# Second layer's attention on one Trainium2 core: scalings behind a tile's exponentials, five output rows begun, token sums behind the last addition

## The chip, the core and the metric

The kernel runs on one core of a Trainium2 chip. A core has a matrix engine (TensorE, PE in the profile, with its weight loads as PEld), a vector engine (VectorE, DVE), an activation engine (ScalarE, ACT), GpSimd (POOL) and a queue for transfers (SyncE, SP). Each takes its own instructions in the order in which the program lists them and waits for the others through semaphores. Matrix products go to PSUM, eight banks of 128 partitions by 512 float32 numbers; everything else that the engines work on lies in SBUF.

The metric is the device time of one execution in microseconds (us). The kernel before takes 1174.16 us, the median of 3 runs (1173.87 to 1174.22).

## What is computed

A trunk of two layers over 512 tokens of width 1024 that also attends to 256 memory tokens. The first layer is a gated DeltaNet, the second a sliding-window attention with one sink logit per head (12 heads of 64, 2 shared key/value heads, window 128). Both layers add the attention to the memory (4 heads), an output projection and a SwiGLU feed-forward block. The change touches the second layer only:

```python
def sliding_window_attention(q, k, v, sinks):
    ...
    s = jnp.where(mask[None, :, None, None], s, -jnp.inf)
    m = jnp.maximum(jnp.max(s, axis=-1, keepdims=True), sink)
    p = jnp.exp(s - m)
    p = (p / (jnp.sum(p, axis=-1, keepdims=True) + jnp.exp(sink - m))).astype(v.dtype)
    o = jnp.einsum("bnhgqk,bnkhd->bnqhgd", p, vw)
...
        x = x + jnp.concatenate([mix_out, mem_o], axis=-1) @ w_out[layer]
        x = x + swiglu(rms_norm(x, ln_ffn[layer]), w_gate_up[layer], w_down[layer])
```

## The kernel before

All activations are kept transposed, as 8 tiles of 128 features by 512 tokens. Each float32 product is made of three products of numbers in a reduced format: a tile is split into a high part (`hi`, `h`, `whi`, a rounding copy on ACT) and a low part (`lo`, `l`, `wlo`, a subtraction on DVE), and `mm3` issues high x high, high x low and low x high. A projection to 128 features is eight `mm3`, so 24 matmuls of 512 columns. Its weights come as one 512 KB transfer into `wraw` (two buffers), which both halves of the split then read.

**The attention tiles** (`swa`, line 1120). Two heads make a tile: tiles 0 to 5 are the windowed heads, 6 and 7 the memory heads. For each tile `queries` projects and rotates the queries, `scores` multiplies them with the keys into PSUM banks `qk` and takes mask and maximum out of them on DVE (line 750), `softmax` makes the exponentials on ACT (line 784) and the reciprocal of their sum `den` (line 787), `weighed` scales the probabilities `sm` by it (lines 805 and 807: of the four token blocks n, the odd ones on ACT, the even ones on DVE), transposes them on PE into PSUM banks `pt`, copies these to `pf`, multiplies them with the values into another `pt` bank `o`, and `split` (line 849) makes the pair `h`, `l` of the result. The loop at line 1205 runs as a software pipeline: in turn t the scores of tile t, the transposes and values of the tile two turns earlier, the exponentials of the tile between, and, cut into pieces of 2, 3 and 4 `mm3` between them, the projection of the queries two turns ahead or, from turn 4 on, the first pieces of an output row.

**The output rows** (`row`, `output`, lines 852 and 862). Row m is one projection of the eight tiles `mix` to features m. Rows 0 to 3 are begun inside the attention (`rows`), in the banks `pj`, `pj` and the two halves of one `qk` tile; each lacks its last piece until tile 5 is done. Rows 4 to 7 run behind them. After each row DVE adds it to the residual `x[m]`, ACT and DVE make the pair `h`, `l` for the feed-forward block, and the squares are accumulated (`sq`, `sqa`).

**The start of the feed-forward block** (`ffn`, line 879). `gate(0)` and a second projection read all eight pairs; two more gates follow. `token_sums` (line 995) makes four sets of sums of the x tiles (`fc`, `raw`, then the split `T`) that `quarters` (line 1019) needs for the rest of the block; for its weights `quarters` also loads `ws` tiles and adds to them by transfers that POOL issues.

**What sets the order.** A scheduler merges the calls into one list per engine, by the order in which they are written and by what each waits for; `nosync` adds an order between two instructions without a semaphore. Pools decide which buffer a tile gets: `pj`, `qk` and `pt` have two each in the second layer's attention, taken in turn, and a new user of a buffer waits for the last reader of the old tile.

Of the kernel before, what the change touches and what calls it, by code (L numbers as in the profile page):

```python
# [85 lines left out]
class Builder:  # L86
    def __init__(self, tc, a):
        self.tc, self.nc, self.a = tc, tc.nc, a
        self.n = 0
        self.valued, self.turned = None, [None, None]  # L90
        self.table, self.table_ins, self.table_users = None, None, []
# [630 lines left out]
    def scores(self, pool, q, kk, win):  # L722
# [6 lines left out]
        mx, den, nm = (self.t(pool, [P, 2 * NC], F32, t, 3 if own else 2) for t in ("mx", "den", "nm"))  # L729
        for n0 in range(0, NC, 2):  # L730
# [14 lines left out]
            for b in range(2):  # L745
                i = b * NC + n0
                if win:
                    for n in (n0, n0 + 1):
                        c0 = 0 if n else P
                        nc.vector.tensor_tensor_reduce(  # L750
                            out=sm[n][:, b, c0:], in0=ps[b][:, n - n0, c0:], in1=self.band[:, c0:], scale=1.0,
                            scalar=NEG, op0=ALU.add, op1=ALU.max, accum_out=mx[:, b * NC + n:b * NC + n + 1])
# [7 lines left out]
        return sm, mx, den, nm  # L760

    def weigh(self, pool, scores, vv, m, out, sinks):
        self.softmax(pool, scores, sinks)
        for _ in self.weighed(pool, scores, vv, m, out, sinks is not None):
            pass

    def softmax(self, pool, scores, sinks):

        nc = self.nc
        win = sinks is not None  # L770
        sm, mx, den, nm = scores
        if win:
# [4 lines left out]
            es = self.t(pool, [P, 2 * NC], F32, "es", 2)  # L777
            self.tt(nc.vector, v4(es), v4(nm), sk, ALU.add)
            self.fn(es, es, AF.Exp)
            for n in range(NC):  # L780
                c0 = 0 if n else P
                for b in range(2):
                    i = b * NC + n
                    self.fn(sm[n][:, b, c0:], sm[n][:, b, c0:], AF.Exp, scale=0.125, bias=nm[:, i:i + 1],
                            accum_out=den[:, i:i + 1])
            self.tt(nc.vector, den, den, es, ALU.add)
        nc.vector.reciprocal(den, den)

    def weighed(self, pool, scores, vv, m, out, win):
# [4 lines left out]
        sm, mx, den, nm = scores  # L794
        o = None if own else self.bank("sc")
        group = NC if own else 2
        for n in range(NC):
# [3 lines left out]
            p = sm[n][:, :, k0 * P:]  # L801
            dn = den.rearrange("p (b n) -> p n b", b=2)[:, n, :]
            for b in range(2):
                if n % 2:
                    ins = nc.scalar.activation(p[:, b], p[:, b], AF.Copy, scale=dn[:, b:b + 1]).ins  # L805
                else:
# [496 lines left out]
```

## Time and profile before

| | |
|---|---|
| median of 3 runs | 1174.16 us |
| the profiled execution, whole | 1174.01 us |
| its span from first to last instruction | 1171.8 us |
| PE busy, DVE busy, ACT busy, POOL busy | 98%, 71%, 54%, 7% |
| second layer's scores to last values | about 696 to 782 us |
| rest of the output rows | about 782 to 809 us |
| feed-forward block of the second layer | from 814 us |

The table's times are from the start of the span. A view by time lists an instruction's start, its length, engine, line, operation and tiles, and in brackets how long its engine had been idle and which instruction of another engine ended that. Ends of matmuls are modelled and overlap the next start, so for PE the distance from start to start is the better measure of what a matmul costs. `PEclk` in a view by stretches is the granted TensorE clock, 1.00 being full speed.

### The profile page before, as it was taken

To read this page: it belongs to the slowest core of one execution; us is meant where nothing else is said; L and a number is where in the kernel's file an instruction comes from. 1 tells how busy PE (TensorE), PEld (TensorE's weight loads), DVE (VectorE), ACT (ScalarE), POOL (GpSimd) and SP (SyncE) were. 2 spreads that over 40 slices of the span, in tenths; PEclk is the share of its full clock that TensorE was granted. 3 is DMA by queue.
4 is the path that set the end of the run, shared out by engine and by line. 5 is a ranking of instruction groups with operands and counts; after the bars stand their busy time and mean duration, and the time that the engine had idled before them with its cause. 6 is when DMAs were issued, how large, how long until landed. Compare 5 with 4: busy or idle time off the path is not lost.

```text
span 1171.8 us, 19281 instructions
## 1 busy us (share of the span) xinstructions
PE 1143.1 (98%) x7330; PEld 995.9 (85%) x7330; DVE 832.6 (71%) x1558; ACT 628.9 (54%) x1250; POOL 83.0 (7%) x93
## 2 busy tenths in 40 slices
PE   7999999999999999999999999998999999999997
PEld 6888777877899998899988786776899988999986
DVE  5654877767788976488955777748798734889644
ACT  7579572366466642266643557844566522566433
POOL 0210000000111101012000000001011000111000
PEclk9999999999999999999999999998999999999998
DMA  8434341324657636377533421116377633676232
GB/s 305 124 111 117 127 118 65 101 79 162 187 136 184 157 109 167 105 180 185 135 86 99 133 65 55 55 30 187 96 183 187 158 99 106 161 176 164 84 99 83
DMA packets 72943, 151.20 MB, mean 129 GB/s; under 512 B 16732, under 2 KB 19444, under 8 KB 72852
## 3 DMA queue, kind: packets, MB, share of 16 engines
q1 hardware_dynamic: 61908, 130.06, 35.5%
q0 software_dynamic: 10944, 19.93, 10.9%
q8 instruction: 57, 0.93, 0.3%
q14 instruction: 34, 0.28, 0.1%
HBM read 143.00 MB, written 6.96 MB: 128 GB/s over the span
## 4 chain that ended last, share of the span: by engine, by line
PE 86%; DVE 8%; ACT 4%; DMA 1%; issue 1%; SPq 0%; DVEq 0%; ACTq 0%
PE pj L144 40%; PE g L144 38%; PE sc L144 5%; DVE wlo L151 2%; ACT sm L132 1%; DVE sm L750 1%; PE qk L144 1%; PE g L148 1%; DMA wraw<-in_wgu 1%; PE pt L144 1%; DMA wraw<-in_wmk 1%; PE pt L148 1%; ACT sm L805 1%; DVE qv L154 1%; DVE q L151 0%
## 5 line engine op out<-in xcount | busy, mean ns | idle before, releaser
L138 ACT ACTIVATE whi<-wraw 128x512 fp32r<-128x512 f32 (+2 forms) x324 | 241.9, 753 | 270.9 <-PE pj L144 162.6
L151 DVE TENSOR_TENSOR wlo<-wraw,whi 128x512 fp32r<-128x512 f32 (+2 forms) x324 | 270.5, 843 | 109.3 <-ACT whi L138 103.9
L144 PE MATMUL pj<-h,whi 128*128 128x512 f32 (+1 forms) x668 | 264.6, 397 | 6.1 <-DVE x L151 5.2
L144 PE MATMUL pj<-l,whi 128*128 128x512 f32 (+1 forms) x668 | 262.3, 393 | 0.0
L144 PE MATMUL pj<-h,wlo 128*128 128x512 f32 (+1 forms) x668 | 261.3, 391 | 0.0
L144 PE MATMUL g<-T,whi 128*128 128x256 f32 x1216 | 220.5, 282 | 0.0
L144 PEld LDWEIGHTS g<-T,whi 128*128 128x128 f32 x1216 | 187.0, 189 | 1.1 <-DVE fu L154 1.1
L144 PE MATMUL g<-T,wlo 128*128 128x256 f32 x608 | 171.1, 281 | 0.0
L144 PEld LDWEIGHTS pj<-h,whi 128*128 128x128 f32 x668 | 125.7, 189 | 35.2 <-issue 9.4
L144 PEld LDWEIGHTS pj<-h,wlo 128*128 128x128 f32 x668 | 126.0, 189 | 26.3 <-issue 0.9
L144 PEld LDWEIGHTS pj<-l,whi 128*128 128x128 f32 x668 | 126.0, 189 | 25.4 <-issue 0.9
L144 PE MATMUL g<-h,whi 128*128 128x256 f32 (+1 forms) x500 | 146.5, 293 | 0.0
L144 PE MATMUL g<-h,wlo 128*128 128x256 f32 (+1 forms) x500 | 145.8, 292 | 0.0
L144 PE MATMUL g<-l,whi 128*128 128x256 f32 (+1 forms) x500 | 145.5, 291 | 0.0
L144 PEld LDWEIGHTS g<-T,wlo 128*128 128x128 f32 x608 | 114.4, 188 | 0.0
L144 PEld LDWEIGHTS g<-h,whi 128*128 128x128 f32 x500 | 95.0, 190 | 2.3 <-issue 0.5
L144 PEld LDWEIGHTS g<-l,whi 128*128 128x128 f32 x500 | 94.9, 190 | 2.3 <-issue 0.5
L144 PEld LDWEIGHTS g<-h,wlo 128*128 128x128 f32 x500 | 95.0, 190 | 1.7
L1028 POOL DMA_DIRECT2D ws<-in_wgu x38 | 33.1, 872 | 744.6 <-ACT h L138 245.2
L138 ACT ACTIVATE whi<-ws 128x512 fp32r<-128x512 f32 x76 | 48.0, 631 | 49.3 <-PE g L144 41.3
L151 DVE TENSOR_TENSOR fu<-pj,rstd 128x512 f32<-128x512 f32 (+1 forms) x34 | 22.4, 660 | 52.8 <-PE pj L144 52.8
L151 DVE TENSOR_TENSOR wlo<-ws,whi 128x512 fp32r<-128x512 f32 x76 | 52.1, 686 | 7.3 <-ACT whi L138 7.2
(375 smaller groups left out, 1666.1 us busy)
## 6 DMA issues: line engine op xcount, KB each, us to landing
wraw<-in_wgu SPq DMA_DIRECT2D x50, 512.0 KB, 4.2
ws<-in_wgu SPq DMA_DIRECT2D x76, 256.0 KB, 3.6
ws<-in_wgu POOLq DMA_DIRECT2D x76, 256.0 KB, 4.8
wraw<-in_win SPq DMA_DIRECT2D x26, 512.0 KB, 3.6
wraw<-in_wdn SPq DMA_DIRECT2D x32, 384.0 KB, 3.1
wraw<-in_wdn SPq DMA_DIRECT2D x32, 320.0 KB, 2.9
wraw<-in_wgu SPq DMA_DIRECT2D x38, 256.0 KB, 4.5
wraw<-in_wout SPq DMA_DIRECT2D x16, 512.0 KB, 3.5
```

The lines of the kernel that those rows point to most:

```text
L132: ins = self.nc.scalar.activation(out, in_, func, **kw).ins
L138: self.copied = self.nc.scalar.activation(out, in_, AF.Copy, **kw).ins
L144: return self.nc.tensor.matmul(out, lhsT, rhs, start=start, stop=stop, skip_group_check=more).ins
L148: return self.nc.tensor.transpose(out, in_, self.ident[:k, :k]).ins
L151: return eng.tensor_tensor(out=out, in0=a, in1=b, op=op).ins
L154: self.nc.vector.scalar_tensor_tensor(out=out, in0=in0, scalar=scalar, in1=in1, op0=op0, op1=op1)
L750: nc.vector.tensor_tensor_reduce(out=sm[n][:, b, c0:], in0=ps[b][:, n - n0, c0:], in1=self.band[:, c0:], scale=1.0, scalar=NEG, op0=ALU.ad ...
L805: ins = nc.scalar.activation(p[:, b], p[:, b], AF.Copy, scale=dn[:, b:b + 1]).ins
L1028: nc.gpsimd.dma_start(s1, a22, accum_op=ALU.add)
```

## The change

It does four things.

1. `softmax` now also takes the reciprocals and issues all scalings (the new method `scale`) right behind a tile's exponentials, instead of `weighed` doing them just ahead of the transposes in the next turn. The small steps between maximum and exponentials (`mx`, `nm`, `es`) move to the end of `scores`.
2. `weighed` no longer splits its result. The new `settle` does it behind the next `softmax`, with the subtraction that makes `l` ordered behind the last scaling on DVE. Exponentials are ordered behind the copies of the transposes (`turned`).
3. Five output rows are begun instead of four: rows 2 and 3 share one `qk` tile, row 4 has half of another, and rows 3 and 4 have weight buffers of their own (`oh`, `ol`). From row 4 on, the weights of the next row are loaded and split ahead of the addition of the present one.
4. The token sums 1 to 3 are ordered behind the last row's addition (`ended`), and the transfers of `quarters` behind the last row's weights (`behind`).

```diff
@@ split and load
-        self.tt(eng or self.nc.vector, lo, src, hi.bitcast(F32), ALU.subtract)
+        self.low = self.tt(eng or self.nc.vector, lo, src, hi.bitcast(F32), ALU.subtract)
...
-        self.nc.sync.dma_start(raw, src)
+        self.loaded = self.nc.sync.dma_start(raw, src).ins
@@ softmax and scale
+            first = self.fn(es, es, AF.Exp)
             for n in range(NC):
                 c0 = 0 if n else P
                 for b in range(2):
                     i = b * NC + n
-                    self.fn(sm[n][:, b, c0:], sm[n][:, b, c0:], AF.Exp, scale=0.125, bias=nm[:, i:i + 1],
-                            accum_out=den[:, i:i + 1])
+                    ins = self.fn(sm[n][:, b, c0:], sm[n][:, b, c0:], AF.Exp, scale=0.125, bias=nm[:, i:i + 1],
+                                  accum_out=den[:, i:i + 1])
+                    self.nosync(ins, first)
+                    if self.turned:
+                        self.nosync(ins, self.turned[n > 1 or n + b > 1])
             self.tt(nc.vector, den, den, es, ALU.add)
         nc.vector.reciprocal(den, den)
+        if "pt" in self.pbufs:
+            for n in range(NC):
+                self.scale(sm, den, n, win)
+
+    def scale(self, sm, den, n, win):
+        p = sm[n][:, :, P if win and n == 0 else 0:]
+        dn = den.rearrange("p (b n) -> p n b", b=2)[:, n, :]
+        for b in range(2):
+            if n % 2:
+                self.copy(p[:, b], p[:, b], scale=dn[:, b:b + 1])
+            else:
+                self.scaled = self.nc.vector.tensor_scalar(
+                    out=p[:, b], in0=p[:, b], scalar1=dn[:, b:b + 1], scalar2=None, op0=ALU.mult).ins
@@ weighed
-            for b in range(2):
-                if n % 2:
-                    ins = nc.scalar.activation(p[:, b], p[:, b], AF.Copy, scale=dn[:, b:b + 1]).ins
-                else:
-                    ins = nc.vector.tensor_scalar(out=p[:, b], in0=p[:, b], scalar1=dn[:, b:b + 1], scalar2=None, op0=ALU.mult).ins
...
+            if not own:
+                self.scale(sm, den, n, win)
...
-        self.split(o, *out)
+        self.ready = o
+        if not own:
+            self.split(o, *out)
@@ output
+        w = None
         for m in range(KD):
-            ps = list(begun[m] if m < len(begun) else self.row(layer, m, mix, lambda: bank(m)))[-1]
-            self.tt(nc.vector, self.x[m], ps, self.x[m], ALU.add)
+            ps = list(begun[m] if m < len(begun) else self.row(layer, m, mix, lambda: bank(m), w))[-1]
+            ahead = bool(begun) and len(begun) <= m + 1 < KD
+            w = self.weight(a["wout"][layer, m + 1]) if ahead else None
+            self.ended = nc.vector.tensor_tensor(out=self.x[m], in0=ps, in1=self.x[m], op=ALU.add).ins
+            if ahead:
+                self.nosync(self.ended, self.low)
...
+        self.behind = self.loaded if layer else None
@@ token_sums
-        self.ts(c, x0[:, q:], g0, ALU.mult)
+        ins = nc.vector.tensor_scalar(out=c, in0=x0[:, q:], scalar1=g0, scalar2=None, op0=ALU.mult).ins
+        if layer and j:
+
+            self.nosync(ins, self.ended)
@@ quarters
-        nc.sync.dma_start(s1, a21)
-        nc.sync.dma_start(s3, a11)
+        for to, part in ((s1, a21), (s3, a11)):
+            ins = nc.sync.dma_start(to, part).ins
+            if self.behind is not None:
+                self.nosync(ins, self.behind)
@@ swa
+        def settle(o, out):
+
+            hi, lo = out
+            self.copy(hi, o)
+            self.nosync(nc.vector.tensor_tensor(out=lo, in0=o, in1=hi, op=ALU.subtract).ins, self.scaled)
...
-        own = dict(pool=sp, tags=("oh", "ol"), bufs=1)
-        rows = [self.row(1, m, mix, (lambda: self.bank("pj")) if m < 2 else (lambda m=m: half(m - 2)),
-                         **(own if m == 3 else {})) for m in range(4)]
+        rows = [self.row(1, m, mix, (lambda: self.bank("pj")) if m < 2 else half,
+                         **(dict(pool=sp, tags=("oh", "ol"), bufs=2) if m > 2 else {})) for m in range(5)]
...
-            beside((6, 7, 0, 1, 2, 3)[t], *(some(work, i) if i < 4 else work for i in n))
+            o = beside((6, 7, 0, 1, 2, 3)[t], *(some(work, i) if i < 4 else work for i in n))
             softmax((7, 0, 1, 2, 3, 4)[t])
-        beside(4, some(rows[0], 2), some(rows[1], 2), some(rows[2], 3))
+            settle(*o)
+        o = beside(4, some(rows[0], 2), some(rows[1], 2), some(rows[2], 3))
         softmax(5)
-        for m, n in ((2, 3), (3, 3)):
+        settle(*o)
+        for m, n in ((2, 3), (3, 4)):
             list(some(rows[m], n))
-        beside(5, some(rows[3], 3), [list(some(rows[m], 1)) for m in range(2)], some(rows[2], 1))
+        settle(*beside(5, some(rows[3], 2), some(rows[4], 3), (next(rows[m]) for m in (4, 4, 4, 0, 1))))
+        for m in range(2, 5):
+            list(some(rows[m], 1))
```

The instructions are the same but for their order. The next listings show it at three places. All three are DVE's list; a row has the line, the operation, the tile written and the tiles read.

The first place is turn 3 of the loop, from the rotation of the last queries (`rs`, `q`) to the subtraction `l` that frees the `pt` bank. Before:

```order
L826 COPY pf_7494<-pt_7489 128x512
L1115 STREAM_SHUFFLE rs_7506<-pj_7446 128x512
L151 TENSOR_TENSOR q_7505<-pj_7446,cosT_2749 128x512
L151 TENSOR_TENSOR rs_7506<-rs_7506,sinT_2750 128x512
L807 TENSOR_SCALAR sm_7287<-sm_7287,den_7290 128x128
L151 TENSOR_TENSOR q_7505<-q_7505,rs_7506 128x512
L151 TENSOR_TENSOR l_7439<-pt_7511,h_7438 128x512
```

After, in the same turn (`ol` and `wlo` are low halves of output weights, `den` the sum of the exponentials):

```order
L838 COPY pf_7502<-pt_7497 128x512
L1142 STREAM_SHUFFLE rs_7514<-pj_7462 128x512
L151 TENSOR_TENSOR q_7513<-pj_7462,cosT_2749 128x512
L151 TENSOR_TENSOR rs_7514<-rs_7514,sinT_2750 128x512
L151 TENSOR_TENSOR den_7302<-den_7302,es_7304 128x8
L151 TENSOR_TENSOR wlo_7818<-wraw_7815,whi_7817 128x1024
L151 TENSOR_TENSOR q_7513<-q_7513,rs_7514 128x512
L794 RECIPROCAL den_7302<-den_7302 128x8
L151 TENSOR_TENSOR ol_7917<-wraw_7914,oh_7916 128x1024
L806 TENSOR_SCALAR sm_7299<-sm_7299,den_7302 128x128 x2
L806 TENSOR_SCALAR sm_7300<-sm_7300,den_7302 128x256 x2
L1213 TENSOR_TENSOR l_7455<-pt_7519,h_7454 128x512
```

Sum, two splits of weights, reciprocal and four scalings now stand between the rotation and `l`. In turns 1 and 2 the list is the same without the row of `ol`.

The second place is behind the last values, where the rows are added to x. Before (`wlo_8006`, `wlo_8046` and `wlo_8086` are the low halves for rows 4, 5 and 6; x_535 is x[0] and so on):

```order
L151 TENSOR_TENSOR wlo_8006<-wraw_8003,whi_8005 128x1024
L154 SCALAR_TENSOR_TENSOR l_7959<-x_535_2732,gains_67,h_7958 128x512
L154 SCALAR_TENSOR_TENSOR l_7969<-x_536_2733,gains_67,h_7968 128x512
L151 TENSOR_TENSOR sqa_7974<-sq_7962,sq_7972 128x512
L154 SCALAR_TENSOR_TENSOR l_7981<-x_537_2734,gains_67,h_7980 128x512
L151 TENSOR_TENSOR x_538_2735<-qk_7817,x_538_2735 128x512
L151 TENSOR_TENSOR sqa_7986<-sqa_7974,sq_7984 128x512
L151 TENSOR_TENSOR wlo_8046<-wraw_8043,whi_8045 128x1024
L154 SCALAR_TENSOR_TENSOR l_7996<-x_538_2735,gains_67,h_7995 128x512
L151 TENSOR_TENSOR sqa_8001<-sqa_7986,sq_7999 128x512
L151 TENSOR_TENSOR x_539_2736<-pj_8009,x_539_2736 128x512
L151 TENSOR_TENSOR wlo_8086<-wraw_8083,whi_8085 128x1024
```

After (ahead of the first row stand x[0], x[1], `wlo_8037` for row 5 and the `l` of x[0]; `wlo_8077` is the low half for row 6):

```order
L889 TENSOR_TENSOR x_537_2734<-qk_7821,x_537_2734 128x512
L154 SCALAR_TENSOR_TENSOR l_8000<-x_536_2733,gains_67,h_7999 128x512
L151 TENSOR_TENSOR sqa_8005<-sq_7993,sq_8003 128x512
L154 SCALAR_TENSOR_TENSOR l_8012<-x_537_2734,gains_67,h_8011 128x512
L889 TENSOR_TENSOR x_538_2735<-qk_7821,x_538_2735 128x512
L151 TENSOR_TENSOR sqa_8017<-sqa_8005,sq_8015 128x512
L889 TENSOR_TENSOR x_539_2736<-qk_7920,x_539_2736 128x512
L154 SCALAR_TENSOR_TENSOR l_8024<-x_538_2735,gains_67,h_8023 128x512
L151 TENSOR_TENSOR sqa_8029<-sqa_8017,sq_8027 128x512
L154 SCALAR_TENSOR_TENSOR l_8042<-x_539_2736,gains_67,h_8041 128x512
L151 TENSOR_TENSOR sqa_8047<-sqa_8029,sq_8045 128x512
L151 TENSOR_TENSOR wlo_8077<-wraw_8074,whi_8076 128x1024
```

Between the low halves of two rows stood at most six other rows, and now between those of rows 5 and 6 stand twelve: the `l` of x[0] and the eleven above.

The third place is the last row's addition (x_542). Before:

```order
L151 TENSOR_TENSOR x_541_2738<-pj_8089,x_541_2738 128x512
L151 TENSOR_TENSOR T_8257<-raw_8250,T_8256 128x1024
L151 TENSOR_TENSOR wlo_8214<-wraw_8211,whi_8213 128x1024
L154 SCALAR_TENSOR_TENSOR l_8116<-x_541_2738,gains_67,h_8115 128x512
L151 TENSOR_TENSOR sqa_8121<-sqa_8081,sq_8119 128x512
L154 SCALAR_TENSOR_TENSOR raw_8261<-x_536_2733,gains_67,fc_8260 128x256
L154 SCALAR_TENSOR_TENSOR raw_8261<-x_540_2737,gains_67,fc_8260 128x256
L154 SCALAR_TENSOR_TENSOR raw_8261<-x_540_2737,minus_8247,raw_8261 128x256
L158 TENSOR_SCALAR fc_8305<-x_537_2734,gains_67 128x256
L151 TENSOR_TENSOR x_542_2739<-pj_8129,x_542_2739 128x512
```

After (`wlo_8174` is the low half for `gate(0)`, `wlo_8214` that for the projection behind it):

```order
L151 TENSOR_TENSOR wlo_8174<-wraw_8171,whi_8173 128x1024
L889 TENSOR_TENSOR x_541_2738<-pj_8089,x_541_2738 128x512
L151 TENSOR_TENSOR wlo_8214<-wraw_8211,whi_8213 128x1024
L154 SCALAR_TENSOR_TENSOR l_8122<-x_541_2738,gains_67,h_8121 128x512
L151 TENSOR_TENSOR sqa_8127<-sqa_8087,sq_8125 128x512
L154 SCALAR_TENSOR_TENSOR raw_8250<-x_539_2736,minus_8247,raw_8250 128x256
L889 TENSOR_TENSOR x_542_2739<-pj_8129,x_542_2739 128x512
L151 TENSOR_TENSOR T_8257<-raw_8250,T_8256 128x1024
L154 SCALAR_TENSOR_TENSOR l_8156<-x_542_2739,gains_67,h_8155 128x512
L151 TENSOR_TENSOR sqa_8161<-sqa_8127,sq_8159 128x512
```

The second set of token sums (`raw_8261`) has left the stretch ahead of the last addition, and the split `T` of the first set stands behind that addition. On SP's list the transfer of the last row's weights has moved from behind four `ws` transfers and one of `wraw` to ahead of them.

More of the change, by code (lines that the diff above doesn't have):

```diff
@@ L89, in __init__ @@
         self.n = 0
-        self.valued, self.turned = None, [None, None]
+        self.valued, self.turned, self.scaled, self.behind = None, [], None, None
         self.table, self.table_ins, self.table_users = None, None, []
@@ L1030, in quarters @@
         last = self.t(fp, [P, T], F32, "wraw", 2)
-        nc.sync.dma_start(last, a22)
+        ins = nc.sync.dma_start(last, a22).ins
+        if self.behind is not None:
+            self.nosync(ins, self.behind)
         pa, pb, pc = (self.bank("g")[:, :q] for _ in range(3))
```

67 lines of the change are left out of this document (33 added, 34 removed).

## Prediction

> **What bounds the kernel now.** I read the page first, then who waited for whom, then the engines' lists in order of time around the longest waits.
>
> ```profile
> PE 1143.1 (98%) x7330; PEld 995.9 (85%) x7330; DVE 832.6 (71%) x1558; ACT 628.9 (54%) x1250; POOL 83.0 (7%) x93
> PE 86%; DVE 8%; ACT 4%; DMA 1%; issue 1%; SPq 0%; DVEq 0%; ACTq 0%
> PE pj L144 <- DVE x L151: 5.2, 1, 5.2
> PE pt L148 <- ACT sm L805: 2.5, 5, 0.6
> ```
>
> PE is busy 98% of the span and is 86% of the chain that ended last. The change leaves its matmuls alone, so it can only give back PE's waits in the second layer's attention and behind it, or add some. The first wait listed is the longest that PE has apart from the start of the program: the matmuls of `gate(0)` wait 5.2 us for an addition to x. PE's list there, the clock in two stretches, and a stretch of the chain in full stream:
>
> ```profile
> 808.35 0.39 PE L144 MATMUL pj<-h,wlo 128*128 128x512 f32 x1
> 813.96 0.77 PE L144 MATMUL pj<-h,whi 128*128 128x512 f32 x1 [5.23 <-DVE x L151]
> ...
> 817.76 0.39 PE L144 MATMUL pj<-h,whi 128*128 128x512 f32 x1
> ```
>
> ```profile
> 810.00:812.00 2.00, 0.00 (x0) 0.00 (x0) 2.00 (x4) 1.13 (x2) 0.00 (x0) 0.68 0.29 43
> 816.00:818.00 2.00, 2.00 (x8) 1.53 (x7) 1.97 (x4) 0.04 (x1) 0.00 (x0) 0.61 0.72 215
> ```
>
> ```profile
> 827.68 10.88 PE pj L144 x48
> ```
>
> 48 matmuls of 512 columns take 10.88 us, 0.227 from start to start. So the hole costs 813.96 - 808.35 - 0.23 = 5.4 us. In the first stretch the granted clock averages 0.68: at full speed until about 810.7, then at half, 2.0 us after the last matmul's end at 808.74. In the second it averages 0.61, so it came back at about 817.5. The nine matmuls from 813.96 to 817.76 took 3.80 us instead of 9 x 0.227 = 2.04: another 1.75 us.
>
> **Term 1, the hole at `gate(0)`.** DVE's rows say why the addition was late:
>
> ```profile
> 808.14 1.23 DVE L151 TENSOR_TENSOR T<-raw,T 128x1024 fp32r<-128x1024 f32 x1 [0.26 <-ACT T L138]
> 809.28 1.22 DVE L151 TENSOR_TENSOR wlo<-wraw,whi 128x1024 fp32r<-128x1024 f32 x1
> ...
> 813.13 0.69 DVE L151 TENSOR_TENSOR x<-pj,x 128x512 f32<-128x512 f32 x1
> ```
>
> The last row was complete at 808.74; a split of token sums, one of weights and other rows stood ahead of its addition. Why does a product wait for the addition at all? By its bank. `pj` tiles take two buffers in turn: eight query projections, two of the keys and values and rows 0 and 1 are twelve. Before, rows 4, 6 and 7 are numbers 13 to 15, so row 7 lies in the first buffer, which `gate(0)` takes. With row 4 in a `qk` bank, rows 6 and 7 are 13 and 14: `gate(0)` then waits for row 6's addition, and needs row 7 only for its last three matmuls, 21 x 0.227 = 4.8 us after its start. The new list has the addition of row 7 ahead of the first `T`. So both the hole, 5.4 us, and the half clock, 1.75 us, go.
>
> What is late next is the weights of `gate(0)`. Bounds are these two:
>
> ```profile
> 794.87 8.08 DMA wraw<-in_wgu
> ...
> wraw<-in_wout SPq DMA_DIRECT2D x1, 512.0 KB, 3.5
> ```
>
> The chain has their transfer at 8.08 us beside the `ws` traffic; one of the same size in the quiet stretch from 735 us takes 3.5. In the new lists it is issued behind the split for row 6, near 796.8 (below), and so lands between 800.3 and 804.9. Then come the high half on ACT, the low half and row 6's addition on DVE (1.0 + 1.2 + 0.6), so `gate(0)` can start between 803.1 and 807.7, while PE arrives at 806.8. Following the lists to the last `l`, the bounds are 0 and 2.1 us. The `ws` transfers now go ahead of it and are mostly through, so I take 0.3.
>
> **Term 2, waits for scaled probabilities.** In the tiles PE waits for the scalings of the same turn:
>
> ```profile
> 704.48 0.40 PE L144 MATMUL pj<-h,whi 128*128 128x512 f32 x1
> 705.39 0.66 PE L148 MATMUL pt<-consts,sm 128*128 128x128 f32 x4 [0.51 <-ACT sm L805]
> ```
>
> ```profile
> PE pt L148 <- ACT pf L138: 0.9, 1, 0.9
> ...
> PE pj L144 <- ACT h L138: 0.7, 1, 0.7
> ```
>
> The five waits for `sm` of the first view (2.5 us) lie here, one in each of five turns, and so do these two, for a copy of transposes queued behind exponentials (at 756) and for the last tile's `h` (at 782): 4.1 us as the view counts. From start to start each costs more: 705.39 - 704.48 is 0.91 where 0.23 would do, 0.68 for a wait put at 0.51. With 0.17 on each of seven, 5.3 us. The scalings now end a turn earlier, and row 4 fills the last wait.
>
> **Term 3, the wait that takes their place.** `l` frees the `pt` bank that the second transposes of the next tile use, and four scalings now stand ahead of it. One turn on PE and DVE's steps:
>
> ```profile
> 729.71 1.75 PE L144 MATMUL pt<-pf,vt 128*64 128x128 f32 x28
> 731.39 1.79 PE L144 MATMUL qk<-ks,q 64*128 64x128 f32 x16
> ...
> 734.61 0.82 PE L148 MATMUL pt<-consts,sm 128*128 128x128 f32 x6
> ```
>
> ```profile
> 718.48 0.73 DVE L1115 STREAM_SHUFFLE rs<-pj 128x512 f32<-128x512 f32 x1
> 719.11 0.68 DVE L151 TENSOR_TENSOR q<-pj,cosT 128x512 f32<-128x512 f32 x1
> ...
> 721.17 1.22 DVE L151 TENSOR_TENSOR wlo<-wraw,whi 128x1024 fp32r<-128x1024 f32 x1
> 722.31 0.69 DVE L151 TENSOR_TENSOR l<-pt,h 128x512 fp32r<-128x512 f32 x1
> ...
> 725.63 0.81 DVE L807 TENSOR_SCALAR sm<-sm,den 128x128 f32<-128x128 f32 x3
> ```
>
> From values to transposes PE takes 4.9 us, and 0.2 more to the second ones: 5.1 from the end of the queries' projection. DVE's list from there, by starts: shuffle 0.6, two products 1.2, sum and split 1.2, q 0.6, reciprocal 0.1, four scalings 0.9, `l` 0.7, some 5.5 with the signals. That is 0.4 to 0.5 us late in turns 1 and 2. In turn 3 a second split (1.14) stands ahead of the scalings, and PE wants them after three matmuls of row 0: 1.5 us, then 0.2 for `l`. Sum 2.6; the bounds are 0, if other waits cover these, and 1.7 in each of six tiles, 10.2. I take 2.6, worked from the rows. Net of term 2 the tiles gain 2.7; following the lists turn by turn I arrive 4.2 us earlier, since some changes between products go too. I take 3.4.
>
> **Term 4, row 6's low half.** The new list has twelve rows between the low halves for rows 5 and 6.
>
> ```profile
> 783.67 2.01 ACT L138 ACTIVATE whi<-wraw 128x1024 fp32r<-128x1024 f32 x2 [1.32 <-PE pj L144]
> 785.58 0.71 ACT L138 ACTIVATE h<-x,gains 128x512 fp32r<-128x512 f32 x1
> ...
> 788.17 0.69 DVE L151 TENSOR_TENSOR sqa<-sq,sq 128x512 f32<-128x512 f32 x1
> 788.77 0.74 DVE L154 SCALAR_TENSOR_TENSOR l<-x,gains,h 128x512 fp32r<-128x512 f32 x1
> 789.43 0.68 DVE L151 TENSOR_TENSOR x<-qk,x 128x512 f32<-128x512 f32 x1
> ```
>
> From the end of row 0: two high halves and the first `h` on ACT 2.65 us, then twelve rows on DVE, five `l` at 0.66, three additions and four sums of squares at 0.60, 7.5 us, then the split 1.2: 11.35. PE has 40 matmuls between row 0's last and that use, so it arrives 41 x 0.227 - 0.39 = 8.9 after that end. It waits 2.4 us, where before it waited for nothing in rows 4 to 7. Bounds 2.0 and 3.5, the latter if row 7's weights, whose high half stands ahead of two `h` on ACT, land 1 us late.
>
> A hole of 2.4 us is longer than the 2.0 after which the clock fell at 810.7. I count the fall again: at most the 1.75 of term 1, at least 0; 1.5.
>
> [...]
>
> **The sum.** 5.4 + 1.75 + 3.4 - 2.4 - 1.5 - 0.3 = 6.35 us off the profiled execution's 1174.01, of which 1171.8 is span: 1167.6 us. The median of the runs, 1174.16, lies 0.15 higher, inside their spread. The feed-forward block behind is a full stream of matmuls in both. Its token sums cost nothing while they end before the `quarters` begin, at 827.68 + 10.88 = 838.6 in the chain, 24.6 us behind the start of `gate(0)`; three sets, each of four rows below 0.7 and a split of 1.2, are at most 12 us of DVE. If that cover went, `quarters` would start later.
>
> **Rivals.**
>
> [...]
>
> (b) `gate(0)` is not freed: its weights land at 804.9, or its bank is row 7's after all. The first costs 2.1 - 0.3 more, the second 2.2 by row 7's later addition: 1169.5 us.
>
> (c) The tiles gain nothing, DVE's longer line eating term 2 whole: 3.4 less, 1171.0 us.
>
> (d) Slower: ACT is held by weights. In turns 2 and 3 the new list has the high halves `oh` of rows 3 and 4 ahead of a copy of transposes and of an `h`, and each transfer starts only when a split frees its `wraw` buffer. At 3.5 us the first holds ACT for 0.9 us and the second not at all. At the 8.08 of term 1 PE waits 4.6 us for the first and 3.8 for the second, and the clock falls once more, 1.75: 10.1 on top of the forecast, 1177.7 us. It decides from 8.7 us on top, a transfer of some 7.4 us. Against it: nothing else is in flight there, and 3.5 was measured in that very stretch.
>
> (e) The change does not do what it says: the waits for scalings stay where they were, as (c) in time.
>
> **Chances.** Forecast 0.45, (a) 0.27, (b) 0.12, (c) and (e) 0.11, (d) 0.05. The range reaches from the best bounds (clock held, tiles 4.2, row six 2.0, weights in time: 1164.7, a little below for the rest) to (c). Faster by over 0.2%, about what a measurement of this kernel can tell from no change, means below 1171.7: forecast, (a), (b) and a part of (c), 0.88; within 0.2% 0.07; slower 0.05.
>
> **What would show it.** PE's 5.2 us wait for x is gone and the clock is 1.00 as `gate(0)` begins; PE waits about 2.4 us for `wlo` in front of row 6 with five additions on DVE ahead of it; no wait of PE for scaled `sm` but one near 743 of over 1 us; a wait of 0.4 for `l` in turns 1 and 2. Wrong would be a wait for `whi` at `gate(0)`, a wait for `oh` weights in the tiles, or a later start of the `quarters`.

## The result and the profile after

The changed kernel took 1168.89 us, the median of 5 runs (1167.55 to 1170.61), beside 1174.22 for the kernel before (5 runs, 1173.87 to 1175.85). The ratio is 0.995, with a 95% interval of 0.9936 to 0.9965: 4 to 7.5 us off. The profiled execution of the changed kernel took 1167.55 us, the lowest of the five, so what it shows is compared with its own time, and differences of an us between executions are taken up below.

The page and the view of PE's waits from 690 to 840 us, after:

```profile
PE 1141.0 (98%) x7330; PEld 996.0 (85%) x7330; DVE 833.6 (72%) x1558; ACT 629.2 (54%) x1250; POOL 82.8 (7%) x93
PE 90%; DVE 5%; ACT 2%; DMA 2%; issue 1%; SPq 0%; DVEq 0%; ACTq 0%
```

```profile
PE pj L144 <- DVE wlo L151: 3.6, 1, 3.6
PE pt L148 <- DVE sm L806: 1.6, 1, 1.6
PE pt L148 <- ACT sm L138: 0.5, 1, 0.5
PE pt L148 <- DVE l L1213: 0.3, 1, 0.3
```

The 5.2 us for x are gone, and so are four of the five waits for scalings, the one for `pf` and the one for the last tile's `h`. In their place stand one of 3.6 us for row 6's low half, one of 1.6 for a scaled tile in turn 3, and two small ones in turns 1 and 2. The chain that ended last passes the rows like this (start, length, engine and what it did):

```profile
785.93 1.23 DVE wlo L151
...
787.17 4.77 DMA wraw<-in_wout
...
792.02 1.06 ACT whi L138
...
794.40 0.68 DVE sqa L151
...
796.35 1.15 DVE wlo L151
...
797.53 17.15 PE pj L144 x68
814.68 6.32 PE g L144 x26
```

The last `pj` step is 68 matmuls without a break: rows 6 and 7 and all of `gate(0)`. PE's list around the new hole, and the clock in three stretches laid on its fall and return (busy time of PE, PEld, DVE, ACT and POOL, then the granted clock):

```profile
793.49 0.40 PE L144 MATMUL pj<-l,whi 128*128 128x512 f32 x1
797.53 0.79 PE L144 MATMUL pj<-h,wlo 128*128 128x512 f32 x1 [3.64 <-DVE wlo L151]
```

```profile
793.80:797.20 3.40, 0.09 (x1) 0.00 (x0) 3.40 (x5) 1.55 (x3) 2.88 (x4) 1.00 0.99 212
797.20:800.60 3.40, 3.06 (x7) 2.48 (x8) 3.40 (x7) 1.24 (x2) 0.00 (x0) 0.50 0.96 151
800.60:804.00 3.40, 3.40 (x16) 2.77 (x15) 1.50 (x4) 0.00 (x0) 0.00 (x0) 1.00 1.02 340
```

The hole costs 797.53 - 793.49 - 0.23 = 3.8 us, and the half clock (800.6 - 797.53) / 2 = 1.5 more. The clock was at half for 3.4 us here (797.2 to 800.6) and for 6.8 before (810.7 to 817.5); "a window" below, and in the expectations, is 3.4 us at half.

To compare kernels I use one stretch of the profiled executions, from the first product of the memory tiles' scores to the first product of the `quarters`. It holds all that the change moves on PE, and ahead of it the lists are the same. Its two ends, before and then after:

```profile
669.69 1.13 PE L144 MATMUL qk<-mk,q 64*128 64x256 f32 x8
838.39 0.28 PE L144 MATMUL g<-h,whi 128*128 128x256 f32 x1
```

```profile
668.80 2.00 PE L144 MATMUL qk<-mk,q 64*128 64x256 f32 x16
831.72 0.28 PE L144 MATMUL g<-h,whi 128*128 128x256 f32 x1
```

168.7 us before, 162.9 after: 5.8 us gained here. Of the span's 6.1 us (1171.8 to 1165.7) another 0.9 lie ahead of the stretch, where nothing was changed and executions differ by themselves (its start is between 668.8 and 671.2 in all the profiles taken, and the profiled execution of the changed kernel has the earliest); behind it 0.6 are lost.

| kernel | median (lowest to highest) | ratio to before, 95% interval | stretch |
|---|---|---|---|
| changed | 1168.89 (1167.55 to 1170.61) | 0.9950 (0.9936 to 0.9965) | 162.9 |
| tiles alone | 1172.58 (1170.55 to 1174.15) | 0.9981 (0.9972 to 0.9990) | 166.3 |
| rows alone | 1171.53 (1170.04 to 1172.58) | 0.9970 (0.9959 to 0.9982) | 165.1 |
| sums last alone | 1173.77 (1171.15 to 1174.42) | 0.9988 (0.9979 to 0.9997) | 168.1 |
| sums free | 1170.08 (1169.35 to 1170.24) | 0.9959 (0.9946 to 0.9971) | 164.1 |
| row 7 in the gate's bank | 1171.32 (1169.56 to 1173.52) | 0.9972 (0.9962 to 0.9982) | 164.5 |
| row 7's high half later | 1169.00 (1166.76 to 1169.79) | 0.9947 (0.9935 to 0.9960) | 161.6 |
| weights two ahead | 1167.38 (1166.19 to 1168.24) | 0.9937 (0.9924 to 0.9951) | 160.0 |
| the same, `ol` later | 1166.44 (1165.23 to 1167.07) | 0.9929 (0.9917 to 0.9942) | 160.1 |
| two ahead, second split later | 1165.71 (1164.08 to 1167.34) | 0.9923 (0.9909 to 0.9937) | 157.7 |
| the same, `T` on POOL | 1168.90 (1165.78 to 1170.64) | 0.9952 (0.9941 to 0.9964) | 157.4 |

The median of before was 1174.2 to 1175.2 beside these. Two more runs of the changed kernel's lists are among the experiments; their stretches are 164.2 and 163.7 us, so one profile's stretch carries about a microsecond of spread.

### The profile page after: what moved, and what is told of

Same layout as the page of the kernel before. It is cut to its first block, busy times and chain, and to the rows that moved or that the text cites. A ratio compares the mean times of both kernels' runs of the same rounds, so it can differ in the third digit from the quotient of the medians.

```text
span 1165.7 us, 19273 instructions
## 1 busy us (share of the span) xinstructions
PE 1141.0 (98%) x7330; PEld 996.0 (85%) x7330; DVE 833.6 (72%) x1558; ACT 629.2 (54%) x1250; POOL 82.8 (7%) x93
## 4 chain that ended last, share of the span: by engine, by line
PE 90%; DVE 5%; ACT 2%; DMA 2%; issue 1%; SPq 0%; DVEq 0%; ACTq 0%
PE pj L144 43%; PE g L144 38%; PE sc L144 5%; PE qk L144 2%; PE pt L148 1%; DVE wlo L151 1%; PE pt L144 1%; DMA wraw<-in_wout 1%; DVE big L151 1%; PE g L148 1%; ACT sm L132 1%; DVE btmp L151 1%; DMA wraw<-in_wmk 1%; DVE qv L154 1%; ACT whi L138 0%
## 5 line engine op out<-in xcount | busy, mean ns | idle before, releaser
L138 ACT ACTIVATE whi<-wraw 128x512 fp32r<-128x512 f32 (+3 forms) x323 | 240.9, 752 | 262.8 <-PE pj L144 166.4
L151 DVE TENSOR_TENSOR wlo<-wraw,whi 128x512 fp32r<-128x512 f32 (+3 forms) x323 | 269.2, 842 | 103.5 <-ACT whi L138 98.1
L144 PE MATMUL pj<-h,wlo 128*128 128x512 f32 (+1 forms) x660 | 258.1, 391 | 3.7 <-DVE wlo L151 3.6
L144 PE MATMUL pj<-h,whi 128*128 128x512 f32 (+1 forms) x660 | 260.9, 396 | 0.1
L144 PE MATMUL pj<-l,whi 128*128 128x512 f32 (+1 forms) x660 | 259.0, 392 | 0.0
```

What stands on the lines that cost most here:

```text
L138: self.copied = self.nc.scalar.activation(out, in_, AF.Copy, **kw).ins
L144: return self.nc.tensor.matmul(out, lhsT, rhs, start=start, stop=stop, skip_group_check=more).ins
L151: return eng.tensor_tensor(out=out, in0=a, in1=b, op=op).ins
```

## The experiments

### The two halves of the change apart

The first kernel has the change's parts 1 and 2 and not the rest:

```diff
-            ahead = bool(begun) and len(begun) <= m + 1 < KD
+            ahead = False
...
-        self.behind = self.loaded if layer else None
...
-            self.nosync(ins, self.ended)
...
-                         **(dict(pool=sp, tags=("oh", "ol"), bufs=2) if m > 2 else {})) for m in range(5)]
+                         **(dict(pool=sp, tags=("oh", "ol"), bufs=1) if m > 2 else {})) for m in range(4)]
...
```

> The changed kernel with parts 1 and 2 alone: scalings and the late settling of a tile, but four begun rows, the weights of a row taken when it starts, and token sums and ws transfers unordered as before. My theory: the tiles gain by themselves about 4 us (5.3 us of waits for scalings gone, 0.9 us of waits for l in turns 1 and 2 come, and no split of ol stands ahead of the scalings of turn 3), and the hole of over 5 us and the half clock at gate(0) stay: about 1170.2 us. Rival 1, the tiles gain nothing since DVE's longer line eats it: 1174. Rival 2, what the tiles gain is lost at gate(0), since its weights and not PE's arrival set the hole: the hole grows to 9 us and the time stays at 1174.

Measured: 1172.58 us, 2.2 us off (1.2 to 3.3), less than the 4 expected. The hole at `gate(0)` stayed:

```profile
810.85 0.77 PE L144 MATMUL pj<-h,whi 128*128 128x512 f32 x1 [4.89 <-DVE x L889]
```

The stretch is 2.4 us shorter, of which the hole and its half clock take 0.4 back (5.0 and 2.5 instead of 5.4 and 1.75), so the tiles give 2.8. Both rivals fall. What the forecast missed is turn 3: its wait was expected to go with the split of `ol`, and without it PE still waits there for 0.60 us for the scaled tile and for 0.89 at the transposes behind it (section on turn 3).

The second kernel has the parts 3 and 4 on top of the kernel before, with scaling and settling as they were:

```diff
...
+        rows = [self.row(1, m, mix, (lambda: self.bank("pj")) if m < 2 else half,
+                         **(dict(pool=sp, tags=("oh", "ol"), bufs=2) if m > 2 else {})) for m in range(5)]
...
+            w = self.weight(a["wout"][layer, m + 1]) if ahead else None
...
+            self.nosync(ins, self.ended)
...
```

> The kernel before with parts 3 and 4 alone: five begun rows, the next row's weights ahead of the addition, token sums and ws transfers held back; scalings and settling as before. My theory: the hole at gate(0) (5.4 us) and its half clock (1.75 us) go, the wait of 3.6 us for row 6's low half comes with about 1.5 us of half clock, and row 4 fills about 1 us of waits around the last tile: 1174.2 - 7.15 + 5.1 - 1 = about 1171 us, with the waits for scalings still in the tiles. Rival, the row 6 wait comes only from the tiles ending earlier: no such wait, 1166.

Measured: 1171.53 us. The wait at `gate(0)` is gone, and the one before row 6 is there without any change to the tiles, with 3.4 us of half clock behind it, so the rival falls:

```profile
799.40 0.75 PE L144 MATMUL pj<-h,wlo 128*128 128x512 f32 x1 [3.36 <-DVE wlo L151]
```

The stretch is 3.6 us shorter; with those of the tiles that is 6.0, beside the 5.8 of the whole change. The two halves add up within the spread of a stretch.

### Why the hole at the gate closed

Three kernels ask whether it was the bank or the order of the token sums. The changed kernel without that order:

```diff
-        if layer and j:
-            self.nosync(ins, self.ended)
```

> The changed kernel without the order of token sums 1 to 3 behind the last addition. My theory: gate(0) no longer waits for row 7 since row 6's bank is the one it takes, so a later row 7 by the 0.3 us of one fc costs nothing: no hole at gate(0), the time stays at about 1168.9 us. Rival: it is the order of the token sums that closed the hole; then a wait for x of several us is back at gate(0), and the time is 1172 or more.

Measured: 1170.08 us, and no wait at `gate(0)`. The stretch is 1.2 us longer than that of the changed kernel, and all of it is clock: the same hole before row 6 (3.8 us) was followed here by 14 products at half speed, which cost 2.9 us instead of 1.5, as in one of the repetitions. In the lists the order had moved one `fc` only. The kernel before with that order alone:

```diff
-            self.tt(nc.vector, self.x[m], ps, self.x[m], ALU.add)
+            self.ended = self.tt(nc.vector, self.x[m], ps, self.x[m], ALU.add)
...
+        if layer and j:
+            self.nosync(ins, self.ended)
```

> The kernel before with only token sums 1 to 3 ordered behind the last addition, four rows begun. My theory: the addition of row 7 comes earlier by three rows of raw (1.2 us) and one fc (0.35), T and the split for the second projection still stand ahead of it, and gate(0) still waits for row 7's bank: the hole goes from 5.4 to about 3.8 us, with a half clock of one or two windows, about 1172.8 us. Rival: the order alone closes the hole: 1168.

```profile
813.02 0.77 PE L144 MATMUL pj<-h,whi 128*128 128x512 f32 x1 [3.97 <-DVE x L151]
```

Measured: 1173.77 us; the hole shrank by 1.2 us, from 5.2 to 4.0, and did not close. The half clock behind it cost 2.4 us instead of 1.75, so 0.6 is left in the stretch. So in the changed kernel the order of the token sums is worth about nothing.

To test the bank I first took one more `pj` buffer between the rows and `gate(0)`:

```diff
         self.behind = self.loaded if layer else None
+        if layer:
+            self.bank("pj")
```

> The changed kernel with one more pj buffer taken (and not used) between the rows and gate(0), so that gate(0) takes the bank of row 7 instead of row 6; no list of any engine changes. My theory of the ring: gate(0) then waits for row 7's addition, which needs PE to end row 7 and 0.7 us of DVE behind it, so PE stands still for 1.3 to 2 us at gate(0) where it waits for nothing now: about 1170.5 us. Rival: the bank isn't what gate(0) waits for; no wait, 1168.9.

Measured: 1168.53 us, and no wait. This did not do what it was meant to: the feed-forward block opens a pool of its own that starts at the first bank, and the buffer that nothing uses turned no ring. Lists and banks were those of the changed kernel, so the run counts as a repetition of it. The last kernel puts the rows elsewhere:

```diff
-        bank = lambda m: self.bank(("pj", "pj", "pt" if begun else "g")[m % 3])
+        bank = lambda m: self.bank("pj" if m == 7 else "pt") if begun else self.bank(("pj", "pj", "g")[m % 3])
```

> The changed kernel with row 6 in a pt bank and row 7 in the first pj bank, which is the one gate(0) takes; the lists of the engines stay but for the names of the banks. (The kernel with an unused pj buffer taken did not do what was meant: gate(0)'s pool is a new one that starts at the first bank, so gate(0) kept row 6's bank, and that run is a repetition of the changed kernel.) My theory of the ring: gate(0) now waits for row 7's addition, so PE stands still at gate(0) from its last matmul of row 7 through DVE's 0.6 us and what stands ahead of it, 1.3 to 2 us, where the changed kernel waits for nothing: 1170.5 to 1171 us. Rival: the bank isn't what gate(0) waits for; no wait there, 1168.9 to 1169.3.

```profile
810.71 0.39 PE L144 MATMUL pj<-h,wlo 128*128 128x512 f32 x1
812.49 0.47 PE L144 MATMUL pj<-h,whi 128*128 128x512 f32 x1 [1.39 <-DVE x L889]
```

Measured: 1171.32 us, with the wait for x back: 812.49 - 810.71 - 0.23 = 1.55 us, where the same lists with row 6 in that bank have none. `gate(0)` waits for the addition of whichever row lies in its bank. That is shown.

### What stands before row 6

The first kernel moves one row on ACT: the high half for row 7, behind the high parts of x[3] and x[4].

```diff
             w = self.weight(a["wout"][layer, m + 1]) if ahead else None
+            if ahead and m == 6:
+                self.nosync(self.copied, self.fifth)
...
+            if m == 4:
+                self.fifth = self.copied
```

> The changed kernel with the high half for row 7 on ACT ordered behind the high parts of x[3] and x[4]. My theory: the excess of the row 6 wait over the predicted 2.4 us comes from ACT waiting for row 7's weights to land at 791.9; with that out of the way DVE runs through and the hole before row 6 falls from 3.8 to about 2.5 us. Then the clock decides: with one more window at half the gain is 1.3 us, 1167.6; if the clock holds at the shorter hole it is 2.8, 1166.1. Rival: DVE's twelve rows alone take the 3.6 us, or DVE waits for squares: nothing gained, 1168.9.

In the changed kernel ACT and DVE stand like this (start, length, engine, operation, and in brackets the idle time before and what ended it):

```profile
792.02 1.06 ACT L138 ACTIVATE whi<-wraw 128x1024 fp32r<-128x1024 f32 x1 [1.67 <-DMA wraw<-in_wout]
792.99 0.70 ACT L138 ACTIVATE h<-x,gains 128x512 fp32r<-128x512 f32 x1
```

```profile
791.46 0.69 DVE L889 TENSOR_TENSOR x<-qk,x 128x512 f32<-128x512 f32 x1
793.73 0.75 DVE L154 SCALAR_TENSOR_TENSOR l<-x,gains,h 128x512 fp32r<-128x512 f32 x1 [1.58 <-ACT h L138]
...
796.26 1.22 DVE L151 TENSOR_TENSOR wlo<-wraw,whi 128x1024 fp32r<-128x1024 f32 x1
```

Of the 3.6 us of PE, 1.58 are DVE waiting for an `h` that stands behind a high half whose weights took 4.77 us to land. With the row moved, PE's list is:

```profile
793.40 0.39 PE L144 MATMUL pj<-l,whi 128*128 128x512 f32 x1
794.81 0.50 PE L144 MATMUL pj<-h,whi 128*128 128x512 f32 x1 [1.01 <-ACT whi L138]
795.14 0.40 PE L144 MATMUL pj<-l,whi 128*128 128x512 f32 x1
796.25 0.50 PE L144 MATMUL pj<-h,wlo 128*128 128x512 f32 x1 [0.70 <-DVE wlo L151]
```

Row 6's first low product starts at 796.25 instead of 797.53, in two waits of 2.1 us together (1.2 and 0.9 by the distances of starts), and the clock stays at 1.00. Theory and size hold, 2.5 expected and 2.1 found. Yet the median, 1169.0 us, is not below the changed kernel's, and the fastest executions, which are the profiled ones, are only 0.8 apart. Of 3.2 us saved at row 6 (1.7 of the hole, 1.5 of the half clock) the stretch keeps 1.3: PE now comes to the last products of `gate(0)` ahead of x[7]'s pair and waits 1.3 there, and products directly behind a wait take 0.33 us from start to start instead of 0.23, some 0.5 in all.

The second kernel takes the weights two rows ahead, so that row 6's low half stands earlier on DVE:

```diff
...
-            ahead = bool(begun) and len(begun) <= m + 1 < KD
-            w = self.weight(a["wout"][layer, m + 1]) if ahead else None
+            ahead = bool(begun) and len(begun) <= m + 2 < KD
+            if ahead:
+                w.append(self.weight(a["wout"][layer, m + 2]))
```

> The changed kernel with the weights of rows 5 to 7 taken two rows ahead instead of one, which puts row 6's low half ahead of two l, one sum of squares and one addition. My theory: the wait of 3.6 us before row 6 and the half clock behind it (together 5.2 us) go, so about 1163.7 us and a clock of 1.00 from the tiles to the feed-forward block. Rival 1, gate(0)'s own weights or its x become the next wait and take most of it back: 1166 to 1168. Rival 2, the half clock near 797 us does not hang on this hole: 1165.

```profile
809.63 0.39 PE L144 MATMUL pj<-h,wlo 128*128 128x512 f32 x1
811.15 0.50 PE L144 MATMUL pj<-h,whi 128*128 128x512 f32 x1 [1.13 <-ACT h L138]
812.24 0.50 PE L144 MATMUL pj<-l,whi 128*128 128x512 f32 x1 [0.59 <-DVE l L154]
```

Measured: 1167.38 us. No wait before row 6 and no half clock, so the second rival falls; but the first is right. `gate(0)` reaches x[7] 2.15 us (1.3 and 0.86) before its pair is ready, since DVE and ACT stand at the weights of the next projection. The stretch gains 2.9 us, about what 5.2 - 2.15 gives.

The third moves that next split behind the last row, on top of this one (`paired` marks the last high part on ACT):

```diff
...
+            w = self.weight(col(f0, 1))
+            if layer and f0 == 0:
+                self.nosync(self.copied, self.paired)
+                self.nosync(self.low, self.ended)
```

> As the kernel with weights two rows ahead, and the split of the weights of the projection behind gate(0) ordered behind the last row's addition (DVE) and its high part (ACT). My theory: the two waits of 1.1 and 0.6 us at the last three matmuls of gate(0), for h and l of x[7], come from DVE and ACT being held by those weights, which land at 805.4; they go, 2.1 us off the 1167.4 of weights two ahead: about 1165.3 us. Rival: the projection's own low half, now behind more rows, is the next wait, or quarters start earlier than the token sums allow and wait longer for fs: 1166.5 to 1167.4.

Measured: 1165.71 us, the best of all: 0.9923 of before, 9 us off. PE waits for nothing between 756 us and the `quarters`, and the stretch is 157.7. But the rival is there too: the `quarters` wait 1.0 us for a copy `fs` on ACT, and the time behind the stretch grows from 333.4 us in the kernel before (its span less 838.4) to 335.1.

The fourth has POOL make the low halves `T` of the token sums, to unload DVE:

```diff
-        hl = self.weight(None, raw=raw, pool=fp, tags=("T", "T"), bufs=8)
+        hl = self.weight(None, raw=raw, pool=fp, tags=("T", "T"), bufs=8, eng=nc.gpsimd if layer else None)
```

> As the kernel with the second projection's split behind the last row, and the four subtractions that make the low halves T of the token sums on POOL instead of DVE. My theory: with PE some 10 us earlier than in the kernel before, DVE has no idle time left ahead of the quarters, and the wait of 1.0 us for fs (with some 0.6 us beside it) is DVE's lateness; four splits of 1.22 us off DVE remove most of it, 1165.7 - 1.2 = 1164.5 us. Rival: a split on POOL takes some 2.7 us (a product of half the size took 1.3 to 1.5 there), so that the last T is late itself: 1165.7 or above.

```profile
L151 POOL TENSOR_TENSOR T<-raw,T 128x1024 fp32r<-128x1024 f32 x4 | 10.4, 2598 | 23.4 <-ACT T L138 23.4
```

```profile
PE g L144 <- POOL T L151: 2.1, 1, 2.1
```

Measured: 1168.90 us. A split takes 2.6 us on POOL, and PE waits 2.1 for the last. The rival is right, and nothing was gained: the profiled execution, at 1165.78 us the fastest of six, has the span of the kernel before it (1164.0 and 1163.9), and the median is 3.2 us higher.

### Turn 3

The kernel with weights two ahead, and the splits of `ol` behind turn 3's scalings:

```diff
+        if kw:
+            self.nosync(self.low, self.mark)
...
+            if t == 3:
+                self.mark = self.scaled
```

> As the kernel with weights two rows ahead, and the subtractions that make ol, the low halves for rows 3 and 4, ordered behind the scalings of turn 3. My theory: the wait of 1.55 us for a scaled tile in turn 3 falls to the 0.3 to 0.5 us of turns 1 and 2, so 1.2 us below the kernel with weights two ahead alone: about 1162.5 us. Rival, DVE's or ACT's line is only as late by other rows, or the splits now stand ahead of something that PE needs in turn 4 or 5: no gain, 1163.7 or above.

In the changed kernel PE waits there once (1.59 us in the kernel with weights two ahead); with `ol` moved it waits twice:

```profile
744.16 0.43 PE L148 MATMUL pt<-consts,sm 128*128 128x128 f32 x2 [1.55 <-DVE sm L806]
```

```profile
744.16 0.43 PE L148 MATMUL pt<-consts,sm 128*128 128x128 f32 x2 [0.61 <-DVE sm L806]
745.48 0.63 PE L148 MATMUL pt<-consts,sm 128*128 128x128 f32 x4 [0.89 <-DVE l L1216]
```

Measured: 1166.44 us and a stretch of 160.1, beside 160.0 with `ol` where it was. So there was no gain, as the rival said, but not for its reason: DVE's line is earlier. Counted from the start of the stretch, the first transposes come 0.96 us sooner (744.16 - 669.73 = 74.43 instead of 745.59 - 670.20 = 75.39), close to the 1.14 of the row taken away. But the edit changed more than was meant. The scheduler made a new order of PE's list too: three products of row 0, which stood between these transposes and the next, now stand behind both, and PE waits 0.89 us for `l`. Whether the old order of PE would have kept the 0.9 us wasn't tried. The kernel of the tiles alone, without `ol` there, has PE's list in the new order and two waits of the same size, 0.60 and 0.89.

### The changed kernel once more

> The changed kernel itself once more, beside the two others: 1168.9 us within 0.7, row 6's wait at 3.6 to 3.8 us. [...]

Measured: 1169.61 us (1167.66 to 1171.06), ratio 0.9955 (0.9943 to 0.9967); the wait before row 6 is 3.1 us by the view (3.3 by the distances of starts), somewhat below what was expected, since row 7's weights took 4.21 us here instead of 4.77. The profiles of these lists show one window at half clock, which cost 1.5 us, or two, which cost 2.8 or 2.9; the times do not fall into two groups that far apart: 1167.66, 1169.04, 1169.61, 1169.72 and 1171.06.

## Why the prediction was right, and where it was off

The forecast of 1167.6 us is 1.3 below the median and 0.05 above the profiled execution; that closeness is partly luck: 0.9 of the profiled gain lie ahead of the stretch, errors of terms cancel, and terms 1 and 4, which were added up, hang on each other.

**Term 1** held. No wait is left at `gate(0)`, so hole and half clock, 7.15 us, went. The cause is the bank, as the prediction put it: the row in the gate's bank decides (1.55 us come back when it is row 7), and the token sums, to which the diff gives as much room, are worth 1.2 us of the hole in the old order and nothing in the new. The 0.3 counted for what is late next was not needed, but only because row 6's hole made PE late. DVE's and PE's rows at the end of `gate(0)`, after:

```profile
812.72 0.75 DVE L154 SCALAR_TENSOR_TENSOR l<-x,gains,h 128x512 fp32r<-128x512 f32 x1 [0.34 <-ACT h L138]
...
814.06 0.39 PE L144 MATMUL pj<-l,whi 128*128 128x512 f32 x1
```

The last `l` is ready 0.6 us before its product. With row 6's hole at 2.1 us and no half clock, PE waits 1.3 us here, as the experiment with row 7's high half shows. So had term 4 come out as small as forecast, a part of it would have been a wait at `gate(0)`, inside the bounds of 0 to 2.1 us.

**Terms 2 and 3** came out near the 3.4 taken: with 7.15 off and 5.3 back for row 6, the stretch's 5.8 leave 4.0 for the tiles and the last values, and the two repetitions leave 4.1 and 3.9 by the same sum. Alone the tiles give 2.8. Turn 3's wait was called at 1.5 and measured 1.55. Of its two causes, the split of `ol` is borne out, since without it the wait for the scaled tile is 0.6; that the rest comes from PE having only three matmuls of row 0 ahead of those transposes, where it has six of a projection in the turns before, wasn't tried. The waits in turns 1 and 2 were put at 0.4 to 0.5 us for `l`. They are 0.3 and 0.5 in the view, the second put down to a scaling on ACT, against the sign that no other wait for a scaled tile would stay; `l` ends there 0.1 us before PE goes on.

**Term 4** had the right place and chain and was mis-sized: 2.4 us taken, 3.8 measured, above the bound of 3.5. The bound's own condition is what happened: row 7's weights took 4.77 us instead of 3.5, ACT's two `h` stood behind their high half, and DVE lost 1.58 us. Six profiles have these rows in this order (changed, rows alone, sums free, the two repetitions, row 7 in the gate's bank): the transfer took 4.21 to 4.94 us, and DVE's idle time was 3.18 or 3.19 less each time, 1.03 to 1.75. By that a transfer of 3.5 us would leave 0.3 and a hole of about 2.5, an estimate near the forecast, so the length of the transfer is what was mis-sized. With the row moved the hole was 2.1. I should have taken the upper bound, since the same list has four `ws` transfers issued right behind these weights; that they slowed it is likely, and wasn't tried apart.

**The half clock** was taken at 1.5 us and is 1.5 in the profiled execution; that the clock would hold in row 6's hole, the 0.27 of (a), did not happen. The reason behind the 1.5, a hole longer than 2.0 us, does not hold, and that the size came out is partly luck. The clock had fallen 2.0 us after the last matmul in the kernel before; it fell 3.3 us after it here, 1.9 in the changed kernel once more and 4.5 with row 7 in the gate's bank. What sets this time was not shown (last section). The half clock costs 2.9 us in the repetition with the unused buffer, where a second window follows (14 products from 797.81 to 803.89, 6.08 us for 3.18), and 2.8 in the other. So the profiled execution, the fastest of five, shows the cheaper case. Yet this does not explain why the median lies 1.3 us above it: both executions have a mean clock of 0.996 on record, and a second window would take 0.0015 off (3.4 x 0.5 of 1166 us), more than the third digit hides. Where the 1.3 lie stays open; the start of the stretch alone differs by up to 2.4 us between profiles.

**The sum** hid errors: row 6 cost 1.4 more than counted, and the tiles and the 0.3 gave back 0.9. **The cover of the `quarters`** is thinner than I said: behind the stretch 0.6 us were lost (0.2 and 0.4 in the repetitions), and the experiments that bring PE there earlier lose up to 1.7, or 3.9 with `T` on POOL. Rivals (b), (c) and (e) fall by the same rows, and (d) by the chain, which has the transfer for `oh` near the 3.5 and far from 7.4 (ACT stood 0.77 us for it, where 0.9 was said):

```profile
730.16 3.78 DMA wraw<-in_wout
```

## What to carry to other kernels

When a wait is taken away, ask which engine's in-order list PE runs into next, and count in the rows that stand ahead of its operand on every engine that they pass, the landing of their transfers included: here an ACT row that waited for weights cost DVE 1.58 us and PE about as much. Here the first product of `gate(0)` waited 1.55 us for the addition that reads its PSUM bank when that was row 7's, and not at all when it was row 6's: where the rows before a stage lie can be worth more than the order of the work. Three fixes in a row each uncovered the next wait of 1 to 2 us, so take the price of a hole as an upper bound on what its fix brings, and do not add up terms that lie one behind the other as if they were apart.

## What the runs showed of the hardware

The granted clock fell to half at some of PE's holes. Cut into stretches of 3.4 us that lie on the fall and return, the kernel before, two runs of the changed lists (the changed kernel once more, and the one with row 7 in the gate's bank), in that order:

```profile
807.40:810.80 3.40, 1.34 (x6) 0.76 (x5) 3.14 (x4) 3.40 (x5) 0.00 (x0) 0.99 0.22 88
810.80:814.20 3.40, 0.24 (x1) 0.27 (x2) 3.40 (x9) 0.68 (x2) 0.00 (x0) 0.50 0.49 154
814.20:817.60 3.40, 3.40 (x9) 2.63 (x10) 3.40 (x5) 1.84 (x3) 0.00 (x0) 0.51 0.32 82
```

```profile
794.00:797.40 3.40, 1.49 (x7) 0.92 (x5) 2.59 (x5) 2.43 (x5) 2.24 (x3) 1.00 0.99 316
797.40:800.80 3.40, 2.18 (x5) 1.79 (x6) 3.40 (x5) 1.24 (x2) 1.26 (x2) 0.52 1.03 163
800.80:804.20 3.40, 3.40 (x9) 2.63 (x9) 2.37 (x7) 0.00 (x0) 0.00 (x0) 0.50 1.01 255
```

```profile
793.40:796.80 3.40, 2.35 (x11) 1.61 (x9) 2.04 (x5) 3.11 (x5) 1.73 (x2) 1.00 1.02 352
796.80:800.20 3.40, 1.00 (x4) 0.86 (x5) 3.40 (x5) 0.63 (x2) 1.76 (x2) 1.00 1.05 164
800.20:803.60 3.40, 3.40 (x9) 2.63 (x8) 3.37 (x8) 0.83 (x2) 0.00 (x0) 0.50 1.03 201
```

In these rows stretches in which PE was busy for 1.34, 1.49 and 1.00 us (39%, 44%, 29%) were followed by half speed; one with 2.35 (69%) was not. At half speed a stretch with 2.18 us (64%) was followed by another, and the 3.06 us (90%) of the changed kernel by full speed. No run varied the busy share, or the place of a hole, by itself, so what makes the clock fall was not shown. In the last kernel it fell 1 us after PE was back at work (799.20 and about 800.2). The shortest of the holes before row 6 that had a fall behind them was the changed kernel's once more, with 3.13 us of PE's idle time; with row 7's high half later, where PE waited 1.01 and 0.70 us, the clock stayed at 1.00. In the profiles a hole of 3.3 to 3.8 us by the distances of starts was followed by one window at half speed (1.5 to 1.7 us lost) or by two (2.8 or 2.9).
